# A four-layer decoder trunk: first loads in pairs, constants fetched later, a run of matmuls on ones at the start, three interleaved up products, and the squares added on VectorE

## The chip, the cores and the metric

The kernel runs on one core of one Trainium2 chip. The metric is device time in microseconds (us), the median of several runs. Engines are named as in the profile: PE is TensorE's matmul, PEld its weight load, DVE is VectorE, ACT is ScalarE, POOL is GpSimd, SP is SyncE. SP computes nothing here: it only issues transfers.

## What is computed

The input x is 512 tokens by 1024 channels in float32. Four residual layers follow each other, each of a token mixer and a gated feed-forward block:

```python
for layer in range(4):
    h = rmsnorm(x, attn_norm[layer])
    # layers 0 and 3: differential attention; 1: stick-breaking; 2: sliding window
    x = x + mixer(h) @ w_o[layer]
    h = rmsnorm(x, ffn_norm[layer])
    u = causal_depthwise_conv3(h @ w_up) + conv_b      # 1024 -> 2 * 2752
    gate, val = split(u)
    x = x + (silu(gate) * val) @ w_down
return rmsnorm(x, final_norm)
```

Every product is taken at nearly full float32 precision from two rounded halves: an operand is split into `hi` (its rounded copy) and `lo` (the rest), and a product is three matmuls, hi by hi, hi by lo and lo by hi.

## The kernel before

**Layout.** Channels lie on the 128 partitions, so x is eight tiles of 128 by 512 floats (`x[0]` to `x[7]`), 256 KB each. The residual x stays in SBUF for the whole program.

**Norms.** The factor 1/rms of a token is not applied before a product. `Norm.split(d)` makes `h_hi[d]` (ACT, L375) and `h_lo[d]` (DVE, L377) from x[d] times the gain; the products run on these, and the factor `r` is applied to their results, in `conv_chunk` (L1229) or `to_qk`. `Norm.square(d)` squares x[d] on ACT (L384) and adds the squares one after the other into `acc` on POOL (L392). `Norm.finish` splits `acc`, has PE sum it over the partitions with a matrix of ones (L416, L417), and `rstd` makes `r`. An attention also wants `r` by column: four PE transposes with the constant `ident` (L425).

**Weights.** `stream` is the list of all weight pieces in the order of use, mostly 256 KB. `w_feed` has SP load the next piece into one of four raw tiles as soon as one is free (L310); `w_split` rounds it on ACT (`w_hi`, L299), takes the rest on DVE (`w_lo`, L302) and gives the raw tile back. There are four `w_hi` and four `w_lo` tiles; `w_done` gives them back when PE has used the piece. Products are three matmuls per 128 by 128 block of weights (`mm3`, L507 to L509), and `product` takes the pieces for one 128-row output in a row.

**Order.** The order of the instructions of each engine is fixed when the program is built. Each piece of work is a generator that asks a small planner (`Clock`) for an engine with an estimated duration and a priority (the lower number first); the planner hands out each engine by its estimates, and the instructions are written in that order. `yield` of a number of nanoseconds delays the rest of a task in the plan, not on the chip. On the chip every engine takes its list in order, and waits where something is not there yet. A change of one estimate or of one task's engine can thus move other work about.

**The start.** x tiles and the first four weight pieces are issued on SP; the planner is told that each takes 750 ns. The gains and five other constants go out on POOL's queue first of all, and after them the one-hot tables from which `setup_tables` makes the relative bias: PE products L722, rows written to DRAM, and the biases read back (L776). `Forms.first` computes the first four products of layer 0 in step, so that each x tile is used by all four as it comes in: 96 matmuls.

**Entry of a feed-forward block.** `out_projection` finishes the eight output tiles of the mixer; `update` (DVE, L1183) adds each to x and starts its split and square. `steps` takes the first two up products in step (`pair`), so that each pair of halves serves both as it becomes ready: six matmuls for each x tile.

**The end.** The last norm comes in two halves of 256 tokens. `way_out` computes `r` for a half and `scaled_out` multiplies x by it in tiles of 128 by 256, two of eight on POOL (L474); `store` issues three stores on SP (L470).

## Time and profile before

| | |
|---|---|
| median of 3 runs | 2354.62 us (2352.57 to 2358.75) |
| the profiled execution | 2359.97 us, of which the traced span is 2358.2 us |
| mean granted clock of PE | 0.992 of full speed |
| busy share of the span | PE 98%, PEld 82%, DVE 67%, ACT 52%, POOL 13% |
| matmuls | 11207 |

The busy share of PE says little by itself: matmuls overlap, and a matmul that is recorded as 0.39 us is followed by the next after 0.23 us where nothing is late. What is lost is read from the distance between the starts of matmuls. In the timeline a line gives the start, the duration, the engine, the line of the kernel, the operation, what it writes and reads, and in brackets the idle time before it with what ended that.

### The profile page before, as it was taken

The page shows a single profiled execution, that of the slowest core. Times are in us where ns is not written, and L with a number is a line of the kernel's source. Part 1 is how long each engine was busy: PE and PEld are TensorE (multiplying, and loading weights), DVE is VectorE, ACT ScalarE, POOL GpSimd, SP SyncE. Part 2 cuts the span into 40 slices and gives each one's busy share as a digit, 9 for nine tenths or more (in the row PEclk, how much of TensorE's full clock was granted, in tenths as well). Part 3 has the DMA queues.
Part 4 walks back from the last instruction along what each step waited for, and adds up shares of the span by engine and source line. Part 5 has one row for each costly group of instructions (what it writes and reads, how often), then busy time and mean ns, then how long its engine had stood idle before and what let it go on. Part 6 is the DMA issues. An engine that isn't in the chain of part 4 may idle for free.

```text
span 2358.2 us, 32627 instructions
## 1 busy us (share of the span) xinstructions
PE 2310.0 (98%) x11207; PEld 1938.5 (82%) x11207; DVE 1577.7 (67%) x2909; ACT 1225.8 (52%) x2413; POOL 317.0 (13%) x352
## 2 busy tenths in 40 slices
PE   8999999999999999999999899999999999999998
PEld 6888788888888788888888778888888887888887
DVE  6788877753389958777336858776336887877624
ACT  4566644543389845454336845444334665545433
POOL 3343200000111010000011320000012343000001
PEclk9999999999999999999999999999999999999999
DMA  5453233333354223333335423333335642333333
GB/s 189 142 157 94 93 98 107 98 93 94 117 143 111 74 72 108 96 106 94 94 107 145 111 83 101 96 108 94 94 114 143 153 137 73 108 99 103 94 95 109
DMA packets 144103, 256.19 MB, mean 109 GB/s; under 512 B 18495, under 2 KB 33503, under 8 KB 143936
## 3 DMA queue, kind: packets, MB, share of 16 engines
q1 hardware_dynamic: 139856, 241.57, 34.7%
q0 software_dynamic: 4080, 12.53, 2.0%
q8 instruction: 88, 1.44, 0.3%
q14 instruction: 79, 0.65, 0.1%
HBM read 212.02 MB, written 2.16 MB: 91 GB/s over the span
## 4 chain that ended last, share of the span: by engine, by line
PE 88%; DVE 5%; DMA 2%; issue 2%; ACT 2%; POOL 1%; SPq 0%; DVEq 0%; POOLq 0%; ACTq 0%
PE ps L508 26%; PE ps L507 26%; PE ps L509 26%; PE ps L570 5%; PE ps L684 2%; DMA ks<-lo 2%; DVE w_lo L302 1%; DVE h_lo L377 1%; PE ps L950 1%; DVE a L804 1%; PE ps L970 1%; PE ps L882 0%; DMA x<-in_x_dram 0%; PE ps L1137 0%; ACT ns L788 0%
## 5 line engine op out<-in xcount | busy, mean ns | idle before, releaser
L299 ACT ACTIVATE w_hi<-w_raw 128x512 fp32r<-128x512 f32 (+2 forms) x775 | 477.7, 617 | 821.8 <-PE ps L508 658.6
L302 DVE TENSOR_TENSOR w_lo<-w_raw,w_hi 128x512 fp32r<-128x512 f32 (+2 forms) x775 | 535.1, 692 | 436.6 <-ACT w_hi L299 424.7
L507 PE MATMUL ps<-h_hi,w_hi 128*128 128x512 f32 x1840 | 723.2, 393 | 5.4 <-ACT h_hi L375 5.2
L508 PE MATMUL ps<-h_lo,w_hi 128*128 128x512 f32 x1840 | 721.3, 392 | 0.9
L509 PE MATMUL ps<-h_hi,w_lo 128*128 128x512 f32 x1840 | 719.1, 391 | 2.8 <-DVE w_lo L302 2.8
L508 PEld LDWEIGHTS ps<-h_lo,w_hi 128*128 128x128 f32 x1840 | 347.1, 189 | 78.7 <-DVE h_lo L377 10.0
L507 PEld LDWEIGHTS ps<-h_hi,w_hi 128*128 128x128 f32 x1840 | 347.3, 189 | 76.1 <-ACT h_hi L375 5.2
L509 PEld LDWEIGHTS ps<-h_hi,w_lo 128*128 128x128 f32 x1840 | 346.8, 188 | 75.6 <-DVE w_lo L302 3.2
L507 PE MATMUL ps<-gh,w_hi 128*128 128x512 f32 (+1 forms) x693 | 265.3, 383 | 0.0
L509 PE MATMUL ps<-gh,w_lo 128*128 128x512 f32 (+1 forms) x693 | 265.1, 383 | 0.0
L508 PE MATMUL ps<-gl,w_hi 128*128 128x512 f32 (+1 forms) x693 | 265.1, 383 | 0.0
L1229 DVE TENSOR_TENSOR ut<-ps,r_bc 128x512 f32<-128x512 f32 x172 | 118.5, 691 | 176.6 <-PE ps L509 176.6
L1234 ACT ACTIVATE y<-ut,c_conv 128x512 f32<-128x512 f32 x172 | 140.1, 815 | 43.7 <-DVE ut L1229 43.7
L392 POOL TENSOR_TENSOR acc<-tmp,tmp 128x512 f32<-128x512 f32 x9 | 11.6, 1293 | 1050.5 <-ACT tmp L384 1046.2
L508 PEld LDWEIGHTS ps<-gl,w_hi 128*128 128x128 f32 x693 | 130.3, 188 | 25.4
L507 PEld LDWEIGHTS ps<-gh,w_hi 128*128 128x128 f32 x693 | 130.3, 188 | 25.4
L509 PEld LDWEIGHTS ps<-gh,w_lo 128*128 128x128 f32 x693 | 130.3, 188 | 25.3
L1236 DVE SCALAR_TENSOR_TENSOR y<-ut,c_conv,y 128x512 f32<-128x512 f32 x172 | 128.6, 747 | 21.4 <-ACT y L1234 21.1
L1237 DVE SCALAR_TENSOR_TENSOR y<-ut,c_conv,y 128x512 f32<-128x512 f32 x172 | 129.3, 752 | 6.1
L570 PE MATMUL ps<-w_hi,h_hi 128*128 128x256 f32 x416 | 119.6, 287 | 0.0
L570 PE MATMUL ps<-w_hi,h_lo 128*128 128x256 f32 x416 | 118.1, 284 | 0.0
L570 PE MATMUL ps<-w_lo,h_hi 128*128 128x256 f32 x416 | 118.1, 284 | 0.0
(187 smaller groups left out, 3233.5 us busy)
## 6 DMA issues: line engine op xcount, KB each, us to landing
w_raw<-in_w_up_dram SPq DMA_DIRECT2D x344, 256.0 KB, 2.6
w_raw<-in_w_qk_dram SPq DMA_DIRECT2D x108, 256.0 KB, 2.9
w_raw<-in_w_down_dram SPq DMA_DIRECT2D x99, 256.0 KB, 2.6
w_raw<-in_w_down_dram SPq DMA_DIRECT2D x99, 192.0 KB, 2.3
qs<-hi SPq DMA_DIRECT2D x128, 128.0 KB, 3.1
w_raw<-in_w_o_dram SPq DMA_DIRECT2D x64, 256.0 KB, 2.6
w_raw<-in_w_v_dram SPq DMA_DIRECT2D x52, 256.0 KB, 2.8
bias<-rows_da POOLq DMA_DIRECT2D x16, 512.0 KB, 5.2
```

The lines of the kernel that those rows point to most:

```text
L299: copy(hi[:, :n], raw[:, :n], AF.Copy)
L302: nc.vector.tensor_tensor(lo[:, :n], raw[:, :n], f(hi[:, :n]), ALU.subtract)
L377: nc.vector.scalar_tensor_tensor(h_lo[d], x[d], g, f(h_hi[d]), ALU.mult, ALU.subtract)
L507: nc.tensor.matmul(ps, wh, xh, start=start, stop=False, **kw)
L508: nc.tensor.matmul(ps, wh, xl, start=False, stop=False, **kw)
L509: nc.tensor.matmul(ps, wl, xh, start=False, stop=stop, **kw)
L570: nc.tensor.matmul(dst, a[:, ts], c[:, j, :], start=k + b + n == 0, stop=k == ND - 1 and n == 2, skip_group_check=True)
L684: nc.tensor.matmul(dst[half], part[:, half, qs], k2[:, half, ks], start=n == 0, stop=n == 1)
L1229: nc.vector.tensor_tensor(u[:, 2:T + 2], ps, r, ALU.mult)
L1234: nc.scalar.activation(y, u[:, 2:T + 2], AF.Identity, scale=cw[:, 2:3], bias=cw[:, 3:4])
L1236: nc.vector.scalar_tensor_tensor(y, u[:, 1:T + 1], cw[:, 1:2], y, ALU.mult, ALU.add)
L1237: nc.vector.scalar_tensor_tensor(y, u[:, 0:T], cw[:, 0:1], y, ALU.mult, ALU.add)
```

## The change

It has five parts. (1) The gains are fetched on ACT's queue; the other constants are fetched on POOL's queue only after a one-element copy there that reads `x[5]`, and the tables and the transposes of the first norm wait for the event `late` in the plan. (2) `begin` issues six weight pieces and six x tiles by turns (four raw tiles of the ring and two more from the pool of layer 0's attention, which do not go back to the ring); `w_feed` issues `x[6]` and `x[7]` behind weight pieces 6 and 7. The planner's estimates for these are 1.32 ns for each column. (3) Nine matmuls of 128 by 128 by 512 on the matrix of ones stand first on PE; nothing reads their result. (4) The first three up products of each feed-forward block are computed in step, each one x tile behind the one before it, and the weight stream is ordered to match. (5) The squares are added on DVE with priority 1; the sums over partitions are planned 400 ns later; the last multiplication by `r` is done on DVE in two instructions of five and three tiles, stored from SP's and ACT's queues.

```diff
--- before.py
+++ after.py
@@ -26,6 +26,7 @@
 NUP = 2 * D_FF // P
 EPS = 1e-6
 NEG = -1e30
+WARM = 9
 BIG = 3.0e38
 BREAK = 2.0 ** 100
 N_BUCKETS = 32
@@ -246,15 +247,13 @@
 
     banks = ring(psp, "ps", 8)
 
-    def load_const(name):
-        ap = A[name]
-        t = place(const, f"c_{name}", tuple(ap.shape))
-        nc.gpsimd.dma_start(out=t, in_=ap)
-        return t
-
+    def const_tile(name):
+        return place(const, f"c_{name}", tuple(A[name].shape))
+
+    gains = const_tile("gains")
+    nc.scalar.dma_start(out=gains, in_=A["gains"])
     pinned = "natural_log_exp_and_others"
     nc.scalar.preload_act_table_set(pinned)
-    gains = load_const("gains")
     eps = place(const, "eps", (P, 1), F32)
     nc.vector.memset(eps, EPS)
 
@@ -283,8 +282,8 @@
         for g in range(ND * ND // 4):
             stream.append(flat(A["w_o"][l, g]))
         for k0 in (0, 4):
-            stream.extend(flat(A["w_up"][l, m, :, k0:k0 + 4]) for m in A["up_order"][:2])
-        for m in A["up_order"][2:]:
+            stream.extend(flat(A["w_up"][l, m, :, k0:k0 + 4]) for m in A["up_order"][:3])
+        for m in A["up_order"][3:]:
             stream_rows(A["w_up"][l, m], KD)
         for m in range(ND):
             stream_rows(A["w_down"][l, m], KF)
@@ -300,7 +299,8 @@
         lo = yield w_lo
         yield dve(n, prio=-3)
         nc.vector.tensor_tensor(lo[:, :n], raw[:, :n], f(hi[:, :n]), ALU.subtract)
-        raws.give(raw)
+        if id(raw) in raws.ids:
+            raws.give(raw)
         ready[i].set((hi, lo))
 
     def w_feed(first):
@@ -308,8 +308,15 @@
             raw = yield raws
             yield dma()
             nc.sync.dma_start(out=raw[:, :stream[i].shape[1]], in_=stream[i])
-            clock.t += DMA_LAT
+            t = clock.t
+            clock.t = t + DMA_LAT
             spawn(w_split(i, raw))
+            clock.t = t
+            if i < ND:
+                yield dma()
+                nc.sync.dma_start(out=x[i], in_=A["x"][:, i, :])
+                clock.t += DMA_LAT
+                norm.chunk(i, slice(0, T))
 
     def w_next():
         used[0] += 1
@@ -335,6 +342,9 @@
     ones_r = place(const, "ones_r", (P, P), F32R)
     nc.vector.memset(acc[:, 0:P], 1.0 / P)
     nc.vector.tensor_copy(ones_r, acc[:, 0:P])
+
+    for _ in range(WARM):
+        nc.tensor.matmul(banks.free[-1][2], ones_r, ones_r.unsqueeze(1).to_broadcast([P, T // P, P]), start=True, stop=True)
     tmps = ring(const, "tmp", 3)
 
     def rstd(ms, r, scale, cols=slice(0, T)):
@@ -388,8 +398,8 @@
             if n == 1:
                 self.first = sq
             else:
-                yield pool_op(T)
-                nc.gpsimd.tensor_tensor(acc, self.first if n == 2 else acc, sq, ALU.add)
+                yield dve(T, prio=1)
+                nc.vector.tensor_tensor(acc, self.first if n == 2 else acc, sq, ALU.add)
                 tmps.give(sq)
                 if n == 2:
                     tmps.give(self.first)
@@ -411,6 +421,7 @@
             copy(acc_h, acc, AF.Copy)
             yield dve(T)
             nc.vector.tensor_tensor(acc_l, acc, f(acc_h), ALU.subtract)
+            yield 400.0
             ms = yield banks
             yield mm(T, T, prio=-9)
             nc.tensor.matmul(ms, ones_r, acc_h, start=True, stop=False)
@@ -419,6 +430,7 @@
             yield from rstd(ms, r_bc, P / D)
             self.r.set(r_bc)
             if column:
+                yield late
                 ps = yield banks
                 yield mm(P, P, P, P, prio=-3)
                 for b in range(NB):
@@ -460,47 +472,53 @@
             tmps.give(sq)
             yield LAT
             yield from rstd(ms, r_bc, P / D, cols)
-            for group in ((0, 1, 2), (3, 4, 5), (6, 7)):
-                yield from self.store(group, cols, n)
-
-        def store(self, group, cols, n):
-            for t in [spawn(self.scaled_out(d, cols, n, d % 3 == 2)) for d in group]:
-                yield t.end
-            yield dma()
-            nc.sync.dma_start(out=out[:, group[0]:group[-1] + 1, cols], in_=xa[:, group[0]:group[-1] + 1, cols])
-
-        def scaled_out(self, d, cols, n, pool):
-            yield pool_op(n) if pool else dve(n)
-            (nc.gpsimd if pool else nc.vector).tensor_tensor(x[d][:, cols], x[d][:, cols], r_bc[:, cols], ALU.mult)
+            for d0, d1, queue in ((0, 5, nc.sync), (5, ND, nc.scalar)):
+                xs = xa[:, d0:d1, cols]
+                yield dve(n * (d1 - d0))
+                nc.vector.tensor_tensor(xs, xs, r_bc[:, cols].unsqueeze(1).to_broadcast([P, d1 - d0, n]), ALU.mult)
+                yield dma() if queue is nc.sync else act(400)
+                queue.dma_start(out=out[:, d0:d1, cols], in_=xs)
 
     ends = []
 
 
     norm = Norm(0)
-    first = n = 0
-    while n < ND:
-        if raws.free and first < n + 1 + (n > 0):
-            raw = raws.free.pop(0)[2]
-            nc.sync.dma_start(out=raw[:, :stream[first].shape[1]], in_=stream[first])
-            clock.t = 750.0 * (n + first + 1) + DMA_LAT
-            spawn(w_split(first, raw))
-            first += 1
-        else:
+
+    def begin(more):
+
+        raw, at = [r[2] for r in raws.free] + more, 2300.0
+        raws.free.clear()
+        for n in range(len(raw)):
+            w = raw[n][:, :stream[n].shape[1]]
+            nc.sync.dma_start(out=w, in_=stream[n])
+            at += 1.32 * w.shape[1]
+            clock.t = at
+            spawn(w_split(n, raw[n]))
             nc.sync.dma_start(out=x[n], in_=A["x"][:, n, :])
-            clock.t = 750.0 * (n + first + 1) + DMA_LAT
+            at += 1.32 * T
+            clock.t = at
             norm.chunk(n, slice(0, T))
-            n += 1
-    clock.free[SP] = 750.0 * (ND + first)
-    clock.t = 0.0
-    spawn(w_feed(first))
-
-    ident = load_const("ident")
+        clock.free[SP] = 900.0 * len(raw)
+        clock.t = 0.0
+        spawn(w_feed(len(raw)))
+
+    ident, subln, sb_mask, conv = (const_tile(n) for n in ("ident", "subln", "sb_mask", "conv"))
     sinks = place(const, "sinks", (P, 16), F32)
-    nc.gpsimd.dma_start(out=sinks, in_=A["sinks"].to_broadcast([P, 16]))
-    subln = load_const("subln")
-    sb_mask = load_const("sb_mask")
-    conv = load_const("conv")
-    clock.free[POOL] = 8000.0
+    late, sign = event(), place(const, "sign", (P, 1))
+
+    def late_consts():
+
+        yield 9000.0
+        yield pool_op(1)
+        nc.gpsimd.tensor_copy(sign, x[5][:, 0:1])
+        for t, ap in ((ident, A["ident"]), (sinks, A["sinks"].to_broadcast([P, 16])), (subln, A["subln"]),
+                      (sb_mask, A["sb_mask"]), (conv, A["conv"])):
+            yield pool_dma()
+            nc.gpsimd.dma_start(out=t, in_=ap)
+        clock.t += DMA_LAT
+        late.set()
+
+    spawn(late_consts())
 
 
     def mm3(ps, wh, wl, xh, xl, start, stop, **kw):
@@ -701,6 +719,7 @@
             nc.gpsimd.dma_start(out=v[0:ap.shape[0], :n], in_=flat(ap) if len(ap.shape) == 3 else ap)
             return t, v[0:ap.shape[0], :n]
 
+        yield late
         t0, onehot_da = yield from const_in("onehot_da", big)
         t1, onehot_sw = yield from const_in("onehot_sw", small)
         tab = place(pool, "tab", (N_BUCKETS + 1, 16), F32)
@@ -1292,19 +1311,24 @@
         def steps():
             e = None
 
-            pair = [(yield banks), (yield banks)]
-            for k0 in (0, 4):
-                ws = [(yield w_next()), (yield w_next())]
-                for j in range(4):
-                    xh, xl = yield norm.parts[k0 + j]
-                    for ps, w in zip(pair, ws):
-                        wh, wl = w_view(w)
-                        yield mm(T, T, T, prio=5)
-                        mm3(ps, wh[:, j, :], wl[:, j, :], xh, xl, k0 + j == 0, k0 + j == ND - 1)
-                for w in ws:
-                    w_done(w)
+            trio, ws = [], [None] * 3
+            for s in range(ND + 2):
+                for p in reversed(range(3)):
+                    k = s - p
+                    if not 0 <= k < ND:
+                        continue
+                    if k == 0:
+                        trio.append((yield banks))
+                    if k % 4 == 0:
+                        ws[p] = yield w_next()
+                    xh, xl = yield norm.parts[k]
+                    wh, wl = w_view(ws[p])
+                    yield mm(T, T, T, prio=5)
+                    mm3(trio[p], wh[:, k % 4, :], wl[:, k % 4, :], xh, xl, k == 0, k == ND - 1)
+                    if k % 4 == 3:
+                        w_done(ws[p])
             for i, m in enumerate(A["up_order"]):
-                ps = pair[i] if i < 2 else (yield from product(KD, norm.parts))
+                ps = trio[i] if i < 3 else (yield from product(KD, norm.parts))
                 clock.t += LAT
                 got = event()
                 spawn(conv_chunk(m, ps, got))
@@ -1340,6 +1364,8 @@
             ol = place(pool, "ol", (P, ND, T), F32R)
             done, last_bank = [event() for _ in range(ND)], event()
             nxt = Norm(2 * l + 1)
+            if l == 0:
+                begin([place(pool, f"w_raw_more{i}", (P, T)) for i in range(2)])
             if l % 3 == 0:
                 tasks = diff_attention(pool, norm, l, l // 3, oh, ol, done, last_bank)
             elif l % 3 == 1:
```

## Rows read from the trace of the kernel before

**Rows 1.** The page's first part: busy time and instructions of each engine.
```profile
PE 2310.0 (98%) x11207; PEld 1938.5 (82%) x11207; DVE 1577.7 (67%) x2909; ACT 1225.8 (52%) x2413; POOL 317.0 (13%) x352
```

**Rows 2.** PE's waits, whole span: in total, times, longest (us).
```profile
PE ps L684 <- DMA ks<-lo: 8.8, 11, 2.6
```

**Rows 3.** Timeline of PE, 0 to 40 us.
```profile
5.17 0.80 PE L507 MATMUL ps<-h_hi,w_hi 128*128 128x512 f32 x1 [5.17 <-ACT h_hi L375]
...
11.67 0.43 PE L509 MATMUL ps<-h_hi,w_lo 128*128 128x512 f32 x1
...
16.48 0.39 PE L509 MATMUL ps<-h_hi,w_lo 128*128 128x512 f32 x1
...
20.60 0.50 PE L509 MATMUL ps<-h_hi,w_lo 128*128 128x512 f32 x1 [2.80 <-DVE w_lo L302]
...
39.19 0.28 PE L570 MATMUL ps<-w_hi,h_hi 128*128 128x256 f32 x1
```

**Rows 4.** Busy time by stretch; last columns PE's granted clock, DMA share, GB/s.
```profile
5.17:11.67 6.50, 6.50 (x14) 4.75 (x15) 3.77 (x6) 4.08 (x8) 2.12 (x5) 1.00 0.96 308
...
21.86:25.18 3.32, 3.32 (x9) 2.57 (x8) 3.32 (x3) 0.56 (x1) 3.21 (x2) 0.52 0.71 205
...
265.40:271.70 6.30, 6.18 (x24) 3.81 (x22) 6.30 (x6) 3.31 (x6) 5.53 (x4) 1.00 0.01 2
```

**Rows 5.** Timeline of all engines, 0 to 12 us.
```profile
1.07 0.23 DVE L337 CAST ones_r<-acc 128x128 fp32r<-128x128 f32 x1
...
4.40 0.72 ACT L375 ACTIVATE h_hi<-x,c_gains 128x512 fp32r<-128x512 f32 x1 [1.38 <-DMA c_gains<-in_gains_dram]
5.15 0.75 DVE L377 SCALAR_TENSOR_TENSOR h_lo<-x,c_gains,h_hi 128x512 fp32r<-128x512 f32 x1 [1.81 <-ACT h_hi L375]
```

**Rows 6.** Groups of instructions, 17 to 21 us: count, busy us, mean ns.
```profile
L302 DVE TENSOR_TENSOR w_lo<-w_raw,w_hi 128x512 fp32r<-128x512 f32 x2 | 3.9, 1994 | 0.0
L392 POOL TENSOR_TENSOR acc<-acc,tmp 128x512 f32<-128x512 f32 x3 | 3.9, 1288 | 0.5 <-ACT tmp L384 0.4
```

**Rows 7.** Timeline of PE, 250 to 276 us, entry of layer 0's feed-forward block.
```profile
260.44 0.39 PE L507 MATMUL ps<-h_hi,w_hi 128*128 128x512 f32 x1
...
264.52 0.39 PE L507 MATMUL ps<-h_hi,w_hi 128*128 128x512 f32 x1
264.97 0.50 PE L508 MATMUL ps<-h_lo,w_hi 128*128 128x512 f32 x1
265.31 0.39 PE L509 MATMUL ps<-h_hi,w_lo 128*128 128x512 f32 x1
...
273.04 0.39 PE L416 MATMUL ps<-acc_h,ones_r 128*128 128x512 f32 x1
273.58 0.50 PE L417 MATMUL ps<-acc_l,ones_r 128*128 128x512 f32 x1 [0.15 <-DVE acc_l L413]
```

**Rows 8.** Groups of instructions, 265.4 to 271.7 us.
```profile
L392 POOL TENSOR_TENSOR acc<-acc,tmp 128x512 f32<-128x512 f32 x4 | 6.5, 1620 | 0.3
L377 DVE SCALAR_TENSOR_TENSOR h_lo<-x,c_gains,h_hi 128x512 fp32r<-128x512 f32 x4 | 6.3, 1628 | 0.0
```

**Rows 9.** Timeline of DVE and then of ACT, 300 to 325 us, steady feed-forward.
```profile
301.35 0.69 DVE L1229 TENSOR_TENSOR ut<-ps,r_bc 128x512 f32<-128x512 f32 x1 [0.98 <-PE ps L509]
301.95 0.68 DVE L302 TENSOR_TENSOR w_lo<-w_raw,w_hi 128x512 fp32r<-128x512 f32 x1
...
301.17 0.63 ACT L299 ACTIVATE w_hi<-w_raw 128x512 fp32r<-128x512 f32 x1 [2.09 <-PE ps L508]
```

**Rows 10.** The tail: DVE's timeline, and DMA throughput in 40 slices of 2351 to 2359 us.
```profile
2351.21 3.16 DVE L474 TENSOR_TENSOR x<-x,r_bc 128x256 f32<-128x256 f32 x6
...
GB/s 0 0 0 0 0 0 0 0 0 0 0 0 179 348 353 343 353 276 272 343 333 343 358 343 338 343 348 323 46 0 0 0 0 0 0 0 0 0 0 0
```

**Rows 11.** Timelines of POOL, 30 to 40 us, and of PE, 60 to 66 us.
```profile
35.98 0.76 POOL L776 DMA_DIRECT2D bias<-rows_da  x1
...
60.93 0.22 PE L684 MATMUL ps<-ks,qs 128*128 128x128 f32 x1
```

## The prediction

> **What bounds the kernel now.** I read the page first. PE is busy for 98% of the span [rows 1], so time can come only from two places: PE's idle or slow stretches, and the ends before its first and after its last matmul. The page does not show slow stretches, since a stretched matmul counts as busy. So I went through PE's timeline and looked at the distance between starts. Between 11.67 and 16.48 us, 21 matmuls of 512 columns follow each other at 4.81 / 21 = 0.229 us, and nothing there is late [rows 3]. That is the measure; everything above it is loss. The loss that this change can reach lies in three places.
>
> *The start.* PE starts at 5.17 and reaches the first value matmul (256 columns) at 39.19 us [rows 3]. Those 34.02 us hold the 96 matmuls of the first four products, 96 x 0.229 = 22.0 us, and 12.0 us of other things. Of these:
> - 14 matmuls take 6.50 us from 5.17 to 11.67 [rows 3, 4], against 3.21: loss 3.29. Most is the clock: the starts are about 0.43 apart, the lower of PE's two levels (1.2 GHz), and return to 0.229 (2.4 GHz) after PE has worked since 5.17. The clock column says 1.00 there, so before its first change it is not to be trusted.
> - From 16.48 to 20.60 stand three distances, 4.12 us against 0.69: loss 3.43. The wait is for a `w_lo` [rows 3]. That L302 was slowed: two of them averaged 1.99 us while three POOL additions ran beside them [rows 6], against 0.68 in a quiet stretch [rows 9].
> - After that wait the clock falls: 8 distances take 3.32 us at a mean granted clock of 0.52 [rows 4], against 1.83: loss 1.49.
> The remaining 3.8 us are table products, sums and transposes, which stay.
>
> *The four feed-forward entries.* At 264.52 the next matmul comes 0.45 later and the one after that 0.34 later, losses of 0.22 and 0.11 [rows 7]. It waits for `h_lo`, and this happens five times at each entry. At 273.04 the second sum waits 0.54 for `acc_l`: 0.31, and 0.11 for the restart [rows 7]. Together 5 x 0.33 + 0.42 = 2.07 us, the same at the other three entries: 8.3 us. The cause stands beside it: DVE is full for all of 265.4 to 271.7 [rows 4], with four `h_lo` of 1.63 us each while four POOL additions take 1.62 each [rows 8]. Apart they are 0.75 [rows 5] and 1.29 [rows 6].
>
> *The tail.* DVE's last eight multiplications (two of them POOL's) and their stores close the span.
>
> **The change, part by part.**
>
> *Additions on DVE.* An addition moved costs DVE one step of 0.60 us, the distance from one 128x512 operation to the next [rows 9]. It removes 1.63 - 0.75 = 0.88 from the `h_lo` that stood beside it [rows 5, 8]. So DVE gains about 0.3 us for each, and at priority 1 the additions come after updates and halves. The Trainium skill (Perfetto Trace Analysis, Optimizing Scalar/DVE Operations) speaks against the move: a saturated DVE should be relieved toward ScalarE or GpSimd. By that rule seven additions come on top of a full engine, 7 x 0.60 = 4.2 us for each entry. The same skill (SBUF — State Buffer, Who interferes with whom) says that a DVE instruction with two SBUF inputs and a GpSimd instruction that reads SBUF take turns, each for its whole length. The doubled `h_lo` beside the lengthened POOL addition agrees with the second, so I weigh the first only as a rival.
>
> *Three products in step.* Each x tile now feeds nine matmuls, 2.06 us, instead of six, 1.37. The update, halves, addition and three quarters of a `w_lo` for one tile are at most 0.60 + 0.66 + 0.60 + 0.45 = 2.3 us of DVE if everything is interleaved, and 1.7 if the additions wait. DVE's head start over PE (in layer 0 the pair ran 18 matmuls from 260.44 before the first wait [rows 7]) covers 0.25 us for each of eight tiles. I take all 8.3 us as gone. Bounds: 0 kept back if this holds, 8.3 if the waits return in other places. The sum's wait, 0.42 of the 2.07, is met by the 400 ns.
>
> *Weights at the entry.* The fifth and sixth weight pieces now wait for the four tiles of the ring: each tile is freed four block products (12 x 0.229 = 2.75 us) before its successor is needed. From PE's release, a split takes from 301.17 to 302.63, 1.46 us [rows 9], and perhaps one more operation of 0.7 on each engine: 2.9 at worst. I take 0; bounds 0 to 0.3 for each of 8 pieces, 2.4.
>
> *First loads, constants, gains.* Six pairs by turns bring each x tile beside its weights; five constants leave the queues; the gains no longer hold the first `h_hi` (1.38 us idle until they landed [rows 5]). In plan and on the chip, `w_lo` pieces come in the order of use, and no POOL addition slows them. Nothing is fetched that was not fetched. One x tile with its weights serves twelve matmuls, 2.75 us at full clock, against two 256 KB loads, which the 308 GB/s of this stretch [rows 4] brings in 1.7 us. So the loads keep ahead, and I take the 3.43 and the 1.49 as gone; bounds 0 and 4.92 kept.
>
> *Wide matmuls on ones.* The ones are ready at 1.30 [rows 5]; nine matmuls at about 0.43 run to 5.3. The first real matmul starts there instead of at 5.17: 0.15 lost. The halves for it are ready at about the same time. Nine of the 14 slow distances are then spent on nothing that counts; 5 x 0.2 = 1.0 remain. Gain 3.29 - 1.0 - 0.15 = 2.1; bounds: 3.1 (no slow ones left), and 0 (the clock rises no earlier than before).
>
> *Held back.* POOL's copy waits for x[5], and behind it in POOL's queue stand five constants, four table loads, and the first biases. Today the first bias is issued at 35.98, and the first score, which needs it, runs at 60.93 [rows 11]. That is 25 us of cover for a queue whose constants the plan now puts behind 9 us instead of first of all, when the score itself moves 7 us earlier. Cost 0; without the cover, each microsecond of delay would hold the scores.
>
> *End.* Five tiles of 256 in one DVE instruction: 128x512 steps by 0.60, so 1280 columns are about 1.45 us, and 768 about 0.9. The chain of DVE ends 0.8 us sooner than the 3.16 of today [rows 10]. But the stores run at 345 GB/s without a gap for some 3.1 us [rows 10], and the first may now start only after five tiles, about 0.5 us later. By the Trainium skill (Trainium Kernel Development and Optimization, Key Constraints) queues of several engines share the same 16 DMA engines, so ACT's queue adds nothing; if it did, the end would come 0.5 us sooner. I take +0.3; bounds -0.5 and +0.6.
>
> *The order made anew.* New estimates and priorities shift the whole plan. In the attention layers PE waits for late halves, softmax and transfers, 8.8 us for `ks` alone [rows 2], and these may come out better or worse. I take 0, bounds -5 and +5.
>
> **Sum.** Start 2.1 + 3.43 + 1.49 = 7.0; entries 8.3; tail -0.3: 15.0 us. The profiled execution goes from 2359.97 to 2345.0. It lies 5.35 above the median of 2354.62, so the median goes to 2339.6.
>
> **Rivals.**
> - *DVE stays the limit of the entries.* For it: DVE is full there. Against: the slow `h_lo` all lie beside POOL additions. Only the start is gained: 2354.6 - 6.7 = 2347.9.
> - *The start is given back.* Layer 0's attention waits for its biases or for a worse order, though 25 us of cover speaks against it: 2354.6 - 8.0 = 2346.6.
> - *The new order also takes waits out of the attention layers*: 5 to 10 us more, about 2332.
> - *Slower: the weight ring.* Eight pieces come late at the trio. The gain is eaten when each costs 15.0 / 8 = 1.9 us, that is when a split takes 2.75 + 1.9 = 4.6 us from PE's release instead of 1.46; at 2.9 us lateness each the time would be 2363. Only a DVE blocked by several operations before it could do that.
> - *The change does nothing*: the nine matmuls do not bring the clock up earlier and the waits move elsewhere, about 2353.
>
> **How the numbers follow.** Forecast 0.60, own range 2334 to 2346; DVE limit 0.12; start given back 0.11; better order 0.08; nothing 0.05; slower 0.04. About 0.3%, 7 us, is what a measurement can tell from no change, so faster means under 2347.6. That takes 0.58 of the first, half of the second (0.06), two thirds of the third (0.07) and the fourth (0.08): 0.79. Within 0.3%: 0.16. Slower: 0.05. The range from 2330 to 2350 takes in the first three cases and most of the fourth, and leaves out less than 2 in 10.
>
> **What would show it.** Right: starts of matmuls at 0.229 from about 7.5 us on, no wait near 17 us, the first value matmul at about 32; no POOL additions and `h_lo` of 0.75 at each entry, PE there at 0.229 throughout; a first score near 54 us. Wrong: waits of L507 to L509 for `w_lo` in the trio, DVE still full with L377 waited for, a granted clock below 1 after the start, a wait of the scores for `bias`, or more idle time before L684 and L882 than now.

## The result, and the profile after

The changed kernel takes 2330.68 us (median, 2328.47 to 2332.76), the kernel before in the same series 2355.02 us: a ratio of 0.9893 (95% interval 0.9876 to 0.9909). That is 24 us faster by the medians and 25 by the ratio. The forecast was 15 us and a range of 2330 to 2350. The direction was right, and the size was not: applied to 2354.62, the median from which the forecast started, the ratio gives 2329.4.

To see where it went, I cut the program at starts of matmuls that both kernels have, each of them a hi by hi matmul: the last one of each out-projection (it reads `oh`), and the first and the last of each down product (they read `gh`). The stretch from the last one of the out-projection to the first one of the down product is an entry with its up products. All lengths are in us, each the difference of two starts in PE's timeline.

| stretch | before | after | difference | forecast |
|---|---|---|---|---|
| start to the end of layer 0's attention | 259.76 | 243.67 | -16.1 | -7.0 |
| attention of layer 1 | 259.79 | 255.76 | -4.0 | 0 |
| attention of layer 2 | 170.34 | 170.95 | +0.6 | 0 |
| attention of layer 3 | 238.38 | 239.06 | +0.7 | 0 |
| four entries with up products | 4 x 237.22 | 4 x 235.05 | -8.7 | -8.3 |
| four down products | 469.2 | 469.2 | 0 | 0 |
| last down matmul to the end of the span | 11.87 | 12.15 | +0.3 | +0.3 |

The spans differ by 27.2 us and the medians by 24.3: the two profiled executions don't stand alike to their medians. A stretch with the same order of PE's instructions also differs from one profiled execution to another: in the table of all runs by up to 1 us in layer 1, 2 us in layer 2, and 4 us in layer 3 and in layer 0's attention. So the 0.6 and 0.7 of layers 2 and 3 can't be told from nothing, while the 16.1 and the 4.0 can.

PE's timeline at the start of the changed kernel:

```profile
1.40 3.92 PE L347 MATMUL ps<-ones_r 128*128 128x512 f32 x9 [1.40 <-DVE ones_r L344]
5.26 0.49 PE L525 MATMUL ps<-h_hi,w_hi 128*128 128x512 f32 x1
6.05 0.50 PE L526 MATMUL ps<-h_lo,w_hi 128*128 128x512 f32 x1 [0.29 <-DVE h_lo L387]
...
8.93 0.51 PE L525 MATMUL ps<-h_hi,w_hi 128*128 128x512 f32 x1
...
9.66 0.50 PE L527 MATMUL ps<-h_hi,w_lo 128*128 128x512 f32 x1
...
23.39 0.39 PE L527 MATMUL ps<-h_hi,w_lo 128*128 128x512 f32 x1
24.39 0.50 PE L427 MATMUL ps<-acc_h,ones_r 128*128 128x512 f32 x1 [0.61 <-ACT acc_h L421]
25.11 0.51 PE L428 MATMUL ps<-acc_l,ones_r 128*128 128x512 f32 x1 [0.22 <-DVE tab L727]
...
32.24 0.39 PE L588 MATMUL ps<-w_hi,h_hi 128*128 128x256 f32 x1
...
54.34 0.22 PE L702 MATMUL ps<-ks,qs 128*128 128x128 f32 x1
```

The wait of 2.80 us and the slow matmuls behind it [rows 3, 4] are gone. The first value matmul comes at 32.24 instead of 39.19, and the first score at 54.34 instead of 60.93 [rows 11], nearly to the number of the forecast. But PE, at full clock from 6 us on, now waits for data at 8.9 and 9.7, and for the sum of the squares at 24.4.

So the start gives 6.95 us, as forecast, and the 9 us that were not forecast lie behind it, between the first value matmul and the end of layer 0's attention. Busy time over that stretch, first before and then after (the third column from the right is PE's granted clock):

```profile
39.19:259.76 220.57, 211.23 (x1183) 183.84 (x1181) 166.53 (x406) 128.75 (x311) 70.15 (x75) 0.98 0.46 132
```

```profile
32.24:243.67 211.43, 208.20 (x1184) 181.97 (x1184) 163.53 (x408) 128.46 (x311) 72.77 (x78) 0.99 0.49 139
```

The entry of layer 0's feed-forward block in the changed kernel, busy time by stretch and then groups of DVE's instructions from 244 to 260 us:

```profile
244.00:249.30 5.30, 5.30 (x25) 4.40 (x24) 5.30 (x10) 3.75 (x7) 0.00 (x0) 1.00 0.33 100
249.30:255.60 6.30, 6.30 (x29) 5.21 (x29) 6.16 (x10) 4.39 (x8) 0.00 (x0) 1.00 0.17 47
```

```profile
L387 DVE SCALAR_TENSOR_TENSOR h_lo<-x,c_gains,h_hi 128x512 fp32r<-128x512 f32 x6 | 4.2, 746 | 0.0
L402 DVE TENSOR_TENSOR acc<-acc,tmp 128x512 f32<-128x512 f32 x6 | 4.1, 690 | 0.3
```

DVE is as full as before, with ten instructions in 6.3 us where it had six [rows 4]. `h_lo` is back at 0.75 us from 1.63 [rows 8], an addition on DVE is recorded at 0.69 us, and PE has no idle time.

The tail: DVE's timeline, and DMA throughput in 40 slices of 2323 to 2331 us.

```profile
2323.83 2.36 DVE L478 TENSOR_TENSOR x<-x,r_bc 128x1280 f32<-128x1280 f32 x2
...
GB/s 123 0 0 0 0 0 0 0 0 0 0 0 0 0 0 0 154 338 364 343 353 333 328 328 358 343 364 338 343 353 358 236 10 0 0 0 0 0 0 0
```

DVE's last piece takes 2.36 us instead of 3.16 [rows 10], as worked out, and the end is 0.3 us later all the same: the stores still run at some 345 GB/s for 3.1 us, and they start later.

### The profile page after: what moved, and what is told of

It reads as the page before. It is cut to its first block, busy times and chain, and to the rows that moved or that the text cites. A ratio compares the mean times of both kernels' runs of the same rounds, so it can differ in the third digit from the quotient of the medians.

```text
span 2331.0 us, 32610 instructions
## 1 busy us (share of the span) xinstructions
PE 2296.2 (99%) x11216; PEld 1938.0 (83%) x11216; DVE 1587.7 (68%) x2963; ACT 1222.5 (52%) x2413; POOL 224.5 (10%) x286
## 4 chain that ended last, share of the span: by engine, by line
PE 90%; DVE 4%; DMA 2%; ACT 2%; issue 1%; SPq 0%; POOL 0%; DVEq 0%; ACTq 0%; POOLq 0%
PE ps L526 27%; PE ps L527 27%; PE ps L525 27%; PE ps L588 5%; PE ps L702 2%; DMA ks<-lo 1%; DVE w_lo L301 1%; PE ps L969 1%; PE ps L989 1%; DVE a L823 1%; DVE ns L803 1%; PE ps L901 0%; ACT ns L807 0%; PE ps L1156 0%; PE ps L1353 0%
## 5 line engine op out<-in xcount | busy, mean ns | idle before, releaser
L301 DVE TENSOR_TENSOR w_lo<-w_raw,w_hi 128x512 fp32r<-128x512 f32 (+2 forms) x773 | 525.9, 681 | 409.3 <-ACT w_hi L298 391.6
L526 PE MATMUL ps<-gl,w_hi 128*128 128x512 f32 (+1 forms) x693 | 265.4, 383 | 0.0
L527 PE MATMUL ps<-gh,w_lo 128*128 128x512 f32 (+1 forms) x693 | 265.4, 383 | 0.0
L525 PE MATMUL ps<-oh,w_hi 128*128 128x512 f32 x256 | 100.9, 394 | 0.4 <-DVE nm L1067 0.4
## 6 DMA issues: line engine op xcount, KB each, us to landing
w_raw<-in_w_up_dram SPq DMA_DIRECT2D x344, 256.0 KB, 2.6
w_raw<-in_w_qk_dram SPq DMA_DIRECT2D x108, 256.0 KB, 3.0
w_raw<-in_w_down_dram SPq DMA_DIRECT2D x99, 256.0 KB, 2.6
w_raw<-in_w_o_dram SPq DMA_DIRECT2D x64, 256.0 KB, 2.7
w_raw<-in_w_v_dram SPq DMA_DIRECT2D x52, 256.0 KB, 2.8
```

The lines of the kernel that those rows point to most:

```text
L301: nc.vector.tensor_tensor(lo[:, :n], raw[:, :n], f(hi[:, :n]), ALU.subtract)
L525: nc.tensor.matmul(ps, wh, xh, start=start, stop=False, **kw)
L526: nc.tensor.matmul(ps, wh, xl, start=False, stop=False, **kw)
L527: nc.tensor.matmul(ps, wl, xh, start=False, stop=stop, **kw)
```

## The experiments

Three theories stand against each other. *Theory 1*: most of the unforeseen 9 us in layer 0's attention and 4 us in layer 1's come from the order of instructions, which the planner wrote anew when an estimate or an engine changed. I call such an order a draw, since nothing in the edit says whether it will be a good one. *Theory 2*: the changed loads, queues and engines shorten those stretches, whatever the order. *Theory 3*, which came up late: the additions on DVE shorten layer 1, whatever the order. What makes them separable is that the planned order can be compared between kernels before a run. With the additions alone, PE's order in layers 1 to 3 is that of the changed kernel and in layer 0 that of before; with the start alone, layers 1 to 3 are those of before and layer 0 is a third order.

All profiled executions, in us; "L0" runs from the start of the span to the end of layer 0's attention, "of it" is its part from the first value matmul on, and the entry is that of layer 0. The table products (L722) stand ahead of the first value matmul in some orders and behind it in others; they take some 2.3 us in all.

| run | L0 | of it | L1 | L2 | L3 | entry | end | ratio to before (95%) |
|---|---|---|---|---|---|---|---|---|
| before | 259.8 | 220.6 | 259.8 | 170.3 | 238.4 | 237.23 | 11.9 | 1 |
| after | 243.7 | 211.4 | 255.8 | 171.0 | 239.1 | 235.05 | 12.2 | 0.9893 (0.9876 to 0.9909) |
| 1 additions alone | 254.1 | 219.5 | 255.8 | 169.6 | 241.0 | 235.05 | 11.9 | 0.9943 (0.9928 to 0.9958) |
| 2 start and end alone | 246.0 | 216.7 | 259.4 | 171.4 | 238.9 | 237.22 | 12.1 | 0.9956 (0.9941 to 0.9971) |
| 3 after, no ones | 242.2 | 209.9 | 256.0 | 171.2 | 237.0 | 235.05 | 12.2 | 0.9890 (0.9873 to 0.9906) |
| 4 after, two products | 245.5 | 213.5 | 255.6 | 169.3 | 237.0 | 235.05 | 12.1 | 0.9894 (0.9878 to 0.9909) |
| 5 after, 205 ns | 249.4 | 217.8 | 255.6 | 170.0 | 238.3 | 235.05 | 12.1 | 0.9922 (0.9899 to 0.9944) |
| 6 after, 195 ns | 242.8 | 211.3 | 255.8 | 169.4 | 237.8 | 235.05 | 12.5 | 0.9881 (0.9839 to 0.9924) |
| 7 before, POOL 16 us | 250.4 | 219.5 | 259.4 | 171.1 | 238.7 | 237.23 | 11.9 | 0.9960 (0.9948 to 0.9973) |
| 8 before, moves 3500 ns | 268.8 | 228.8 | 267.8 | 175.1 | 235.5 | 237.22 | 11.8 | 1.0098 (1.0075 to 1.0121) |
| 9 third product alone | 260.3 | 223.0 | 259.7 | 169.1 | 237.8 | 237.81 | 11.9 | 1.0018 (1.0007 to 1.0029) |
| 10 after, no 400 ns | 246.1 | 211.7 | 256.6 | 171.1 | 238.7 | 235.05 | 12.1 | 0.9898 (0.9876 to 0.9920) |
| 11 additions, POOL 16 us | 247.8 | 212.1 | 255.7 | 170.9 | 238.1 | 235.05 | 11.8 | 0.9896 (0.9881 to 0.9910) |
| 12 after, 195 ns, no ones, old end | 243.3 | 210.7 | 255.8 | 169.1 | 238.6 | 235.06 | 11.8 | 0.9888 (0.9872 to 0.9904) |
| 13 before, 195 ns | 249.3 | 211.3 | 257.7 | 172.0 | 231.9 | 237.22 | 11.9 | 0.9944 (0.9915 to 0.9973) |
| 14 before, 205 ns | 256.2 | 215.9 | 257.4 | 171.9 | 234.5 | 237.22 | 11.8 | 0.9978 (0.9965 to 0.9992) |
| 15 before, 400 ns alone | 259.7 | 221.0 | 259.5 | 171.7 | 232.2 | 236.79 | 11.8 | 0.9971 (0.9957 to 0.9984) |

In layer 0's attention runs 1, 9 and 15 have the PE order of before, and runs 3, 4 and 10 that of the changed kernel. The first order takes 219.5 to 223.0 us there, the second 209.9 to 213.5.

**1. The additions alone**, on the kernel before, with the 400 ns:

```diff
-                yield pool_op(T)
-                nc.gpsimd.tensor_tensor(acc, self.first if n == 2 else acc, sq, ALU.add)
+                yield dve(T, prio=1)
+                nc.vector.tensor_tensor(acc, self.first if n == 2 else acc, sq, ALU.add)
...
+            yield 400.0
             ms = yield banks
```

> The kernel before with one part alone: squares added on DVE, sums planned 400 ns later. Its order of PE instructions in layer 0's attention is that of before, in the attentions of layers 1 to 3 that of the changed kernel. Theory 1 (the order that the planner writes decides what PE waits for): layer 0's attention as before, layer 1's 4.0 us shorter, layers 2 and 3 about 0.6 us longer each; the four entries lose most of their 2.07 us even without the third product; in all 7 to 11 us faster, ratio 0.9955 plus or minus 0.001. Theory 2 (the earlier start and the emptied queues shorten the attentions, the order is a bystander): attentions as before, only the entries gain, 4 to 8.3 us, ratio 0.9975.

13 us faster, a little over theory 1's range. The entries are at 235.05, all of the changed kernel's gain, with two products. Layer 1 is at 255.8 as in the changed kernel; layers 2 and 3, at 169.6 and 241.0, are not each 0.6 longer as expected, but differ by no more than one order does between executions. The wait of the start is gone with the old loads too: L0 is 5.7 us shorter, and 3.43 + 1.49 = 4.9 of it are the wait and the slow matmuls behind it that the prediction priced. What is left of layer 0 keeps the two long waits of its order. First the kernel before, PE's timeline in layer 0's attention:

```profile
103.71 0.28 PE L684 MATMUL ps<-ks,ql 128*128 128x128 f32 x1
106.60 0.30 PE L684 MATMUL ps<-ks,qs 128*128 128x128 f32 x1 [2.61 <-DMA ks<-lo]
...
108.17 0.63 PE L507 MATMUL ps<-h_hi,w_hi 128*128 128x512 f32 x1
...
189.87 0.49 PE L882 MATMUL ps<-c_ident,a 128*128 128x128 f32 x3
192.92 1.33 PE L882 MATMUL ps<-c_ident,a 128*128 128x128 f32 x5 [2.56 <-DVE a L804]
```

then the kernel with the additions alone:

```profile
102.31 0.45 PE L685 MATMUL ps<-ks,qs 128*128 128x128 f32 x1 [3.92 <-DMA ks<-lo]
...
104.50 0.63 PE L508 MATMUL ps<-h_hi,w_hi 128*128 128x512 f32 x1
...
190.29 0.77 PE L883 MATMUL ps<-c_ident,a 128*128 128x128 f32 x5 [2.58 <-DVE a L805]
```

and the changed kernel, where the worst waits of the stretch are these:

```profile
113.93 0.38 PE L901 MATMUL ps<-c_ident,a 128*128 128x128 f32 x2
115.17 0.30 PE L702 MATMUL ps<-ks,qs 128*128 128x128 f32 x1 [0.86 <-DMA ks<-lo]
...
176.22 0.33 PE L901 MATMUL ps<-c_ident,a 128*128 128x128 f32 x1 [0.41 <-DVE a L823]
177.48 0.33 PE L901 MATMUL ps<-c_ident,a 128*128 128x128 f32 x1 [0.94 <-DVE a L823]
```

The same order waits at the same two instructions, 2.6 to 3.9 us each; the other order does not. Behind these waits in the kernel before the matmuls are recorded at 0.63 us, at the lower clock, so such a wait costs more than its own length. Its granted clock around the second one:

```profile
189.00:200.00 11.00, 8.44 (x43) 7.91 (x42) 7.32 (x18) 3.90 (x10) 5.14 (x5) 0.69 0.71 203
```

**2. Start and end alone**: in the changed kernel the two edits of experiment 1 are taken back, and the three products in step (`trio`) as well.

```diff
-            trio, ws = [], [None] * 3
+            pair = [(yield banks), (yield banks)]
...
-                nc.vector.tensor_tensor(acc, self.first if n == 2 else acc, sq, ALU.add)
+                nc.gpsimd.tensor_tensor(acc, self.first if n == 2 else acc, sq, ALU.add)
```

> The changed kernel without the additions on DVE, the 400 ns and the third product: the new start, the late constants, the matmuls on ones and the new end. PE's order in layers 1 to 3 is that of before; in layer 0 it is a third one. Theory 1: 7 us at the start, entries and attentions 1 to 3 as before, the attention of layer 0 somewhere within 5 us of before's, since its order is neither the one nor the other. Theory 2: 7 us at the start and the same 9 us in layer 0's attention as the changed kernel, 16 us in all, ratio 0.993.

L0 is 13.8 us shorter: 7 expected at the start, and 6.8 more in an order of its own, neither 0 nor 9, and over the 5 that theory 1 allowed. By itself this run does not decide. The entries and layer 1 are those of before (237.22, 259.4). In layer 1 it waits 1.11 us for `ol` before the same score as the kernel before, while the additions-alone kernel and the changed kernel both wait 2.14 for `t`:

```profile
801.37 0.45 PE L951 MATMUL ps<-ks,qs 128*128 128x384 f32 x1 [2.14 <-DVE t L935]
```

```profile
790.97 0.44 PE L969 MATMUL ps<-ks,qs 128*128 128x384 f32 x1 [2.14 <-DVE t L953]
```

(the first of the additions alone, the second of the changed kernel). The waits come with the order, to the hundredth.

**3. Without the ones**:

```diff
-    for _ in range(WARM):
-        nc.tensor.matmul(banks.free[-1][2], ones_r, ones_r.unsqueeze(1).to_broadcast([P, T // P, P]), start=True, stop=True)
```

> The changed kernel without the nine matmuls on ones; the order of all other instructions stays. If they are worth what the prediction says, the first value matmul comes 2.1 us later (0 to 3.3), the rest of the program keeps its lengths, ratio to the changed kernel 1.001. If a cold clock at the start also lengthens what follows (the rival), more than 3.3 us.

No loss: 0.9890 against 0.9893, and the first value matmul at 32.35 against 32.24. PE's timeline without the ones:

```profile
5.17 0.79 PE L521 MATMUL ps<-h_hi,w_hi 128*128 128x512 f32 x1 [5.17 <-ACT h_hi L381]
...
10.82 0.41 PE L521 MATMUL ps<-h_hi,w_hi 128*128 128x512 f32 x1
...
24.93 0.39 PE L523 MATMUL ps<-h_hi,w_lo 128*128 128x512 f32 x1
25.16 0.39 PE L423 MATMUL ps<-acc_h,ones_r 128*128 128x512 f32 x1
25.39 0.39 PE L424 MATMUL ps<-acc_l,ones_r 128*128 128x512 f32 x1
...
32.35 0.38 PE L584 MATMUL ps<-w_hi,h_hi 128*128 128x256 f32 x1
```

The clock rises at 10.8 instead of about 6, as meant. But with the ones PE first runs ahead of its data (at 6.05, 8.93 and 9.66). The last matmul ahead of the first sum still starts 1.5 us sooner (23.39 against 24.93), and there PE waits for the squares: the first sum is issued 0.8 us sooner, the second 0.3 (25.11 against 25.39), the first value matmul 0.1.

**4. Two products in the changed kernel** (the diff of experiment 2, first half). PE's order in the attentions stays.

> The changed kernel with two up products in step instead of three; PE's order in all four attentions stays that of the changed kernel. If the POOL additions were what slowed the entries, each entry stays within 0.5 us of the changed kernel's, 0 to 2 us in all. If DVE was simply too full (the rival), six matmuls for each tile are too few cover and the waits for h_lo come back, up to 1.65 us at each entry, 6.6 us in all.

The entries stay at 235.05. With the additions on DVE, six matmuls for each tile are cover enough; the third product is worth nothing.

**5 and 6. Another draw of the changed kernel**, by one delay that the planner assumes, and 195.0 in the second:

```diff
-LAT = 200.0
+LAT = 205.0
```

> The changed kernel with one estimate of the planner moved, 205 ns instead of 200 for the delay behind an engine. Nothing is computed, loaded or placed otherwise; only the order that the planner writes is another one in all four attentions. Theory 1 (the order is a draw): the attentions of layers 0 and 1 differ by several us from the changed kernel's 211.4 and 255.8, in either direction, and each lies somewhere between 208 and 222, and 254 and 261. Theory 2 (the change itself relieves these stages): both stay within 1.5 us of the changed kernel's.

> The same with 195 ns: a second draw. Theory 1: again other lengths, the spread of the two draws and the changed kernel over 3 us in layer 0 or layer 1. Theory 2: within 1.5 us.

L0 is 249.4 and 242.8 against 243.7: a spread of 6.6 us with nothing changed but a delay in the plan. The first lies 5.7 us behind the changed kernel, with a wait of 2.95 us for an `at1l` that the changed kernel does not have; its attention, at 217.8, is outside the 209.9 to 213.5 of the changed kernel's order. The second, at 211.3, is inside and can't be told from it. Layer 1, however, is at 255.6 and 255.8, not another length: theory 1's "layers 0 and 1" holds for layer 0 alone.

**7. Another draw of the kernel before**:

```diff
-    clock.free[POOL] = 8000.0
+    clock.free[POOL] = 16000.0
```

> The kernel before with one estimate moved: the planner takes POOL as taken up until 16 us instead of 8. PE's order changes in layer 0's attention alone; in layers 1 to 3 it is that of before. Theory 1: layer 0's attention with the start leaves before's 259.8 us by more than 2 us, and the two long waits (ks at 103.7, L882 at 189.9) stand elsewhere or are gone; layers 1 to 3 as before, 259.8 for layer 1. Theory 2: 259.8 within 2 us for the start and layer 0's attention.

9.4 us off L0, 8 us off the total, by one number in the plan that touches layer 0 alone. The two long waits are gone; the longest of the attention is 1.68 us. Theory 2 expected L0 within 2 us and is wrong here. But most of the 9.4 us stands at the start: the first value matmul comes at 30.86 instead of 39.19, of which 2.3 us are table products moved behind it, and the wait for `w_lo` is short:

```profile
17.56 0.50 PE L509 MATMUL ps<-h_hi,w_lo 128*128 128x512 f32 x1 [0.82 <-DVE w_lo L302]
```

Of the attention's 9 us this run shows some 3: 219.5 us with those 2.3 us of table products in it, against 220.6 without.

**8. A truer estimate**:

```diff
-            clock.t += DMA_LAT
+            clock.t += 3500.0
             self.hi.give(hi)
```

> The kernel before with one estimate nearer to what the trace shows: the planner takes 3500 ns instead of 2200 for the moves of the halves of q and k, which land after 2.8 to 6.0 us. If the waits for ks come from that estimate, PE's 8.8 us of waits for ks fall below 4 us, and the attentions of layers 0 and 3 are shorter by 4 us or more together. If the order is a mere draw, these waits go down but others come, and the sum may go either way.

Slower by 1%. The waits for `ks` went, as expected; in their place came 9.1 us for `a` and others, and the attentions of layers 0 and 3 are 6 us longer together. (In layer 0 of the kernel before these moves land after 2.2 to 6.0 us, 3.1 in the median.) A better single estimate did not make a better order.

**9. The third product alone**, on the kernel before (the first half of experiment 2's diff the other way round, with the weight stream to match):

> The kernel before with three up products in step and nothing else; the additions stay on POOL, and PE's order in all four attentions is that of before. If the POOL additions alone hold the entries back, DVE still yields one h_lo each 1.7 us, but nine matmuls now take 2.06: the waits for h_lo go (1.65 us of each entry, 6.6 in all) and only the wait for the sum, 0.42, may stay; ratio 0.997. If the third product is of no use (the rival, as the run with two products hints), the entries stay at 237.2.

Slower, 1.0018. Both theories named there fail: the waits for `h_lo` go, and one for a weight comes. PE's timeline at the entry of layer 0:

```profile
269.99 0.39 PE L508 MATMUL ps<-h_lo,w_hi 128*128 128x512 f32 x1
272.84 0.50 PE L509 MATMUL ps<-h_hi,w_lo 128*128 128x512 f32 x1 [2.46 <-DVE w_lo L302]
```

and its groups of instructions from 265 to 275 us:

```profile
L377 DVE SCALAR_TENSOR_TENSOR h_lo<-x,c_gains,h_hi 128x512 fp32r<-128x512 f32 x5 | 7.4, 1535 | 0.0
```

DVE's instructions, still lengthened by POOL's additions, keep it from `w_lo` until PE already waits. In layers 2 and 3 the matmuls behind this wait are recorded at the lower clock too, and those entries take 239.4.

**10. Without the 400 ns** in the changed kernel:

> The changed kernel without the 400 ns ahead of the sums. PE's order in the attentions of layers 0, 1 and 3 stays. If the 400 ns meet the wait for acc_l, each entry gets up to 0.42 us longer, 1.7 in all; if the faster additions already do, nothing.

The entries stay at 235.05. But L0 is 2.4 us longer, all of it ahead of the first value matmul, which comes at 34.40 instead of 32.24. The sum now stands earlier in PE's list, PE waits longer for it, and in the profiled execution the clock falls behind that:

```profile
24.25 0.51 PE L426 MATMUL ps<-acc_h,ones_r 128*128 128x512 f32 x1 [1.29 <-ACT acc_h L421]
...
27.20 0.63 PE L524 MATMUL ps<-h_hi,w_hi 128*128 128x512 f32 x1
```

So the 400 ns are of use at the start and not at the entries.

**11. Additions, and one number of the plan**: experiments 1 and 7 together, without the new loads, the ones, the third product or the new end.

> The kernel before with the additions on DVE and the 400 ns, and the planner told that POOL is taken up until 16 us: neither the new loads, nor the ones, nor the third product, nor the new end. PE's order in layers 1 to 3 is that of the changed kernel, in layer 0 a new draw. Theory 1: entries 235.05, layer 1 at 255.8, start and layer 0's attention by the draw, 242 to 254; a good draw brings it within 3 us of the changed kernel. Theory 2 (the new start is what the changed kernel gains in layer 0): it stays at 254 and 11 us behind, 2342.

0.9896: not to be told from the whole change. L0 is 247.8, 4 us behind the changed kernel's and 12 us ahead of before's. The draw happens to be the changed kernel's: from the first value matmul on, PE's list in layer 0 is the same but for two groups, of 14 and 3 matmuls, that stand elsewhere. And it takes as long, with the old loads:

```profile
35.65:247.77 212.12, 208.19 (x1187) 181.93 (x1185) 163.05 (x408) 129.08 (x311) 70.89 (x77) 0.99 0.50 140
```

The 4 us stand ahead of it: the first value matmul comes at 35.65 instead of 32.24, after a wait of 1.38 us for a `w_hi` and a stretch at the lower clock.

**12. The best of the terms**: the changed kernel with 195 ns, without the ones, with the old end.

> The changed kernel with the estimate of 195 ns, without the nine matmuls on ones and with the end of before. Orders as in the run with 195 ns. By the single terms: 195 ns about 1.5 us, the ones 0 to 0.5, the end 0.3: 2328, ratio to before 0.988; no more than 0.001 better than the changed kernel, and it may be within what can be told apart.

0.9888 with a median of 2329.69 us: no better than the changed kernel by more than can be told. The end is 11.8, the end's 0.3 us taken back.

**13 to 15. Layer 1, with the additions on POOL in three new orders**: the kernel before with 195 ns, with 205 ns (the diff of experiments 5 and 6), and with the 400 ns alone.

> The kernel before with 195 ns for the planner's delay behind an engine; additions on POOL, another order in all four attentions. Theory 1 (all draws): layer 1's attention falls anywhere between 254 and 262, start and layer 0's between 242 and 265. Theory 3 (the additions on DVE shorten layer 1's attention whatever the order): layer 1 stays at 258 or more, since the additions are on POOL; entries 237.2 by either.

> The same with 205 ns, a second draw. Theory 1: layer 1 anywhere between 254 and 262, not again 259.6. Theory 3: 258 or more in both.

> The kernel before with the sums over partitions planned 400 ns later and nothing else; additions on POOL. Layer 0's order is that of before, those of layers 1 to 3 are new. Theory 1: layer 1 anywhere between 254 and 262. Theory 3: 258 or more. Entries up to 0.42 us shorter each if the 400 ns are of use there.

Layer 1 is at 257.7, 257.4 and 259.5. It moves with the order, and twice below theory 3's 258, but it stays over the 255.6 to 256.6 of the nine kernels with the additions on DVE (which have three orders there among them). The trace speaks against a direct effect of the additions: in the kernel before, all of PE's waits in this attention stand between 802 and 820 us, and POOL has no addition anywhere near them. These two follow each other:

```profile
618.89 1.29 POOL L392 TENSOR_TENSOR acc<-acc,tmp 128x512 f32<-128x512 f32 x1 [1.50 <-ACT tmp L384]
...
873.41 1.30 POOL L392 TENSOR_TENSOR acc<-tmp,tmp 128x512 f32<-128x512 f32 x1 [52.47 <-ACT tmp L384]
```

Experiment 13 gains 13 us, as much as the additions alone, by one number of the plan, most of it in L0 (249.3) and layer 3 (231.9). It decides for layer 0: with the loads and the additions of before, its attention takes 211.3 us, as long as the changed kernel's 211.4. One of the two long waits is left, and the clock holds:

```profile
37.96:249.30 211.34, 205.09 (x1183) 180.10 (x1181) 163.64 (x406) 127.70 (x311) 71.42 (x75) 1.00 0.47 138
```

```profile
106.16 0.30 PE L684 MATMUL ps<-ks,qs 128*128 128x128 f32 x1 [2.58 <-DMA ks<-lo]
106.29 0.28 PE L684 MATMUL ps<-ks,ql 128*128 128x128 f32 x1
106.41 0.44 PE L507 MATMUL ps<-h_hi,w_hi 128*128 128x512 f32 x1
```

Experiment 15 keeps before's order in layer 0 and its L0 (259.7 against 259.8). It shortens each entry by 0.43: with slow additions the 400 ns do at the entries what was expected of them, with fast ones there is nothing left to do there.

## Why the prediction was wrong

The step that failed is the term *"The order made anew"*, with its *"I take 0, bounds -5 and +5"*. In the profiled pair it was worth about -12, beyond its bound: layer 0's attention was 9 us shorter, layer 1's 4.0, and layers 2 and 3 were 0.6 and 0.7 longer. That the order did it is shown for layer 0: the kernel before in another order, with nothing else changed, has the changed kernel's length (experiment 13), and so has the changed kernel's order with the old loads (experiment 11), while the order of before keeps its length with the additions on DVE (experiment 1). For layer 1 it is what remains, since the start (experiments 2 and 7) does not move it and no addition stands near its waits. The sums of the other terms came out, and what happened is the third of the prediction's rivals: the new order also takes waits out of the attention layers, about 2332, to which it gave a chance of 0.08.

I had the waits for `ks` at 8.8 us in all [rows 2] and left out two things: that the order of before holds two waits of over 2.5 us in layer 0's attention alone, with slow matmuls behind them, and that a single layer moves by 10 us. The runs give the true size of the bound: with the additions on POOL and the loads of before, five orders put L0 at 249.3 to 268.8, while the three kernels with before's order, and the loads and additions of before, lie at 259.7 to 260.3. The kernel before stood near the bad end of these draws, so a new order was more likely a gain than a loss; its two long waits showed that, and I did not use them.

Point by point:
- *Additions on DVE, three products*: 8.3 forecast, 4 x 2.17 = 8.7 measured. It is the additions alone (experiments 1, 4, 9 and 10). The rival taken from the Trainium skill (Perfetto Trace Analysis, Optimizing Scalar/DVE Operations), to relieve a full DVE toward GpSimd, would have cost 4.2 us an entry; the entries got 2.2 shorter. The prediction made more of that section than it says: there the move may make sense, and the next sentence warns that work moved between these two might not help, since they share a read port of SBUF. The rule of the Trainium skill (SBUF — State Buffer, Who interferes with whom), by which a DVE instruction with two SBUF inputs and a GpSimd one that reads SBUF take turns, agrees with `h_lo` at 0.75 instead of 1.63. The prediction's 1.29 us for an addition on its own is right, but its rows 6 don't show it, since two lengthened `w_lo` stood beside those three; a row that does is in the last section.
- *Weights at the entry*: 0 taken, and right with the additions on DVE. With them on POOL the third product makes PE wait 2.46 us for a weight (experiment 9): the mechanism of the slower rival exists, and the additions on DVE are what keeps it away.
- *First loads*: the sum of 7.0 came out as 6.95, which is in part luck. The 4.9 of the wait and the clock went as named, but the 2.1 of the ones did not come, and other things made up for it. The 4.9 come with the additions alone (experiment 1), and with the new loads alone as well (experiment 2 has no such wait). But the additions do not see to it in every order: experiment 11 has them and the old loads, and waits and slows again. The *ones* were mis-sized: 2.1 forecast, 0.1 measured (experiment 3), because the prediction did not ask what PE would wait for next, and that was the sum of the squares. Of the 2.0 that remain beside the 4.9, some 0.8 is one pair of table products (L741, two matmuls of 384 columns), which now stands behind the first value matmul instead of before it: its time is not saved but moved. I have not split the rest.
- *Held back*: no score waits for a bias; right.
- *End*: +0.3 forecast and measured. The Trainium skill (Trainium Kernel Development and Optimization, Key Constraints) agrees: two queues gave no more than the 345 GB/s of one.

How much of L0 the new loads give beside the order, experiment 11 answers nearly: with the additions on DVE and almost the same order, the old start costs 3.4 us ahead of the first value matmul and nothing that can be told behind it. Left open is why the orders planned with the additions on DVE come out some 2 us shorter in layer 1 than those planned with them on POOL: the two groups do not overlap there, but there are only a few orders in each, and no run held the order and moved the additions alone.

## What to carry to other kernels

When a program's order comes from a planner's estimates, any edit that touches an estimate can redraw it, in one layer or in all. Look for the longest waits of the present order, take the redraw as a term with bounds from draws that change nothing else, compare edits only where the order is the same, and see first how much one order differs from run to run. An engine that looks full may be slowed by another one's instructions: before its work is moved away, see whether its instructions are longer than the same ones elsewhere in the trace.

## What the runs showed of the hardware

A POOL addition and a DVE instruction with two inputs in SBUF lengthen each other: `h_lo` goes from 0.75 us to 1.63, the addition from 1.29 to 1.62 [rows 5, 8]. The update L1183, which reads one of its inputs from PSUM, stands beside the same additions and keeps its length. In the kernel before, an addition with nothing on DVE beside it, and DVE's instructions beside additions:

```profile
559.17 1.29 POOL L392 TENSOR_TENSOR acc<-acc,tmp 128x512 f32<-128x512 f32 x1 [13.44 <-ACT tmp L384]
...
263.14 0.67 DVE L1183 TENSOR_TENSOR x<-x,ps 128x512 f32<-128x512 f32 x1
263.74 1.18 DVE L377 SCALAR_TENSOR_TENSOR h_lo<-x,c_gains,h_hi 128x512 fp32r<-128x512 f32 x1
```

With the additions on DVE itself ten of its instructions, additions included, fit in 6.3 us where six had stood beside four POOL additions.
